# A norm worked out per 128 tokens behind bank-by-bank products, and a weight split moved by one tile

## The chip, the cores and the metric

The kernel runs on one core of a Trainium2 chip. Its time is the device time of one launch in microseconds (us); the median of three runs of the kernel before is 2459.11 us. Engines are called PE (matrix products, with its weight loads shown apart as PEld), DVE (vector), ACT (scalar activations), POOL (GpSimd) and SP (which issues most loads).

## The reference

Two transformer blocks over 256 tokens of 1024 features, all in float32. The parts that matter here are the norms that follow a product, and what reads the normed rows:

```python
def rms_norm(x, g):
    xf = x.astype(jnp.float32)
    y = xf * lax.rsqrt(jnp.mean(xf * xf, axis=-1, keepdims=True) + EPS)
    return (y * g.astype(jnp.float32)).astype(x.dtype)

def layer_norm_2(x, g, b):
    xf = x.astype(jnp.float32)
    mu = jnp.mean(xf, axis=-1, keepdims=True)
    var = jnp.mean(jnp.square(xf - mu), axis=-1, keepdims=True)
    return ((xf - mu) * lax.rsqrt(var + LN_EPS) * g.astype(jnp.float32) + b.astype(jnp.float32)).astype(x.dtype)
...
        h = h + rms_norm(merged @ w_out[i], g_mix_post[i])     # first block, then its FFN
...
        h = layer_norm_2(DN_ALPHA * h + mix, ln_mix_g[i], ln_mix_b[i])   # second block, twice
        ffn = peer_ffn(h, peer_w_q[i], peer_sub_keys[i], peer_u[i], peer_v[i])
        h = layer_norm_2(DN_ALPHA * h + ffn, ln_ffn_g[i], ln_ffn_b[i])
```

`mix` is a retention mixer in the first layer and a latent attention in the second. `peer_ffn` multiplies its input by a query weight, picks experts by product keys, and sums their rows.

## The kernel before

**Products.** Each float32 operand is split into a high half (rounded, made by ACT, line 150, tile `whi` for weights) and a low half (the rest, made by DVE, line 165, tile `wlo`); a product is three matrix multiplications. Weights come as 797 units of 128x1024 in the order of `PLAN`; SP loads them four ahead, and helpers issue the halves ahead of their use: `issue_hi` up to a limit the high half, `issue_split` the low half too, `run_ahead(1)` the low half of the next unit. The order of instructions on each engine is the order in which the Python code issues them; every engine works through its own list in that order.

**Two kinds of product.** `lin_tm` gives rows of tokens: two blocks of 128 tokens, two banks of 512 features each, so four banks, `psb[b][h]`. With `apart=True` (the products `w_out`, `r_o`, `p_v0`, `m_o`, `p_v1`) the last two weight units are multiplied bank by bank: block 0's two banks, then block 1's, six multiplications a bank. Then `issue_hi(use+2)` issues one more high half (not for `w_out` and `p_v1`), `after(psb)` works out the norm, and `keep_warm` gives PE 17 idle multiplications (line 294). `lin_fm` gives tiles of 128 features by 256 tokens; with `head=2` the first two weights are multiplied tile by tile of the input, as the input is produced, and only from the third weight on one weight at a time.

**The norm.** `LnTail.after` (lines 467 to 472) calls `ln_coeffs`: statistics of the four banks (DVE, line 392), two aggregations (394), then `rstd_root` for both blocks at once: root on ACT (368), variance plus epsilon on DVE (369), the next high half by `ahead` on ACT, reciprocal (377) and a Newton step of three operations (378 to 380), the shift `nm` (405). Then DVE scales block 1 (471) and ACT block 0 (472), half by half. `RmsTail.after` (788 to 793, for `w_out`) is the same with sums of squares by ACT (413), their addition on DVE (415), and no shift. The closing norm in `after1` (1619 to 1637, for `p_v1`) already goes block by block, with both halves of each scaled by ACT (1631); after it come gains on DVE (1635), shifts on POOL for block 0 and on DVE for block 1 (1636), and four stores (1637).

**What follows.** Behind `r_o` and `m_o` stands a query stage (`p_q0`, `p_q1`): PE transposes the normed rows tile by tile (423), ACT applies gain and shift (`rows`, 477), DVE casts the high half (`split`, 483; for tile 5 ACT does, 481) and takes the low half (484), PE multiplies by two weights. Once tile 3 (`HS`) is multiplied, `run_ahead(1)` issues the third weight's low half on DVE; by then `split` of tile 5 has been issued. Behind `p_v0` stands `m_in`, a `lin_tm` fed in the same way.

Of the kernel before, what the change touches and what calls it, by code (L numbers as in the profile page):

```python
# [10 lines left out]
F32 = mybir.dt.float32  # L11
# [4 lines left out]
AF = mybir.ActivationFunctionType  # L16
ALU = mybir.AluOpType
AX = mybir.AxisListType

P = 128  # L20
T = 256
D = 1024
KD = D // P
EPS1 = 1e-6
EPS2 = 1e-5
# [58 lines left out]
WRM = 17  # L84
WR0 = 17

HS = {"p_q0": 3, "p_q1": 3}
HA = (5,)
RSCH = ((1, 0, (0, 1, 2)), (2, 4, (4, 5, 6)), (3, 8, (8, 9, 10)))
SK = 6  # L90
GH = 1
@with_exitstack
def fused_kernel(ctx: ExitStack, tc: tile.TileContext, a: dict, out: bass.AP):
    nc = tc.nc
# [48 lines left out]
    def issue_hi(limit):  # L143
        while st["hi"] < min(limit, len(units)):
            j = st["hi"]
            issue_dma(j + 1)
            n, i, c = units[j]
            if (n, i) not in F4:
                hi = wst.tile([P, 1024], F32R, tag="whi", name=f"whi{j}", bufs=AHEAD + 1)
                nc.scalar.activation(out=hi[:, :c], in_=raws[j][:, :c], func=AF.Copy)  # L150
                his[j] = hi
            st["hi"] += 1
# [143 lines left out]
    def lin_tm(name, x_of, nk, ncol=1024, i0=0, budget=0.0, mid=None, after=None, psb=None, each=None, lead=0, warm=0, apart=False):  # L296

        if psb is None:  # L300
            psb = [[bank(0), bank(1)], [bank(2), bank(3)]]
        for k in range(nk - 2 if apart else nk):
            w = take(name, i0 + k) if k < lead else weight(name, i0 + k, budget)
            if each:
                each(k)
            if mid and k == nk - 2:
                mid(psb)
            if after and k == nk - 1:
                table_ready()
            for b in range(2):  # L310
                xs = x_of(k, b)
                for h, ps in enumerate(psb[b]):
                    tm_half(w, ps, 512 * h, *xs, ncol, k == 0, k == nk - 1)
        if apart:
            ks = (nk - 2, nk - 1)
            ws = []
            for k in ks:
                ws.append(take(name, i0 + k) if ws else weight(name, i0 + k, budget))
                if each:
                    each(k)  # L320
            mid(psb)
            table_ready()
            for b in range(2):
                for h, ps in enumerate(psb[b]):
                    for k, w in zip(ks, ws):
                        tm_half(w, ps, 512 * h, *x_of(k, b), ncol, False, k == nk - 1)
            if name not in ("w_out", PLAN[-1][0]):
                issue_hi(st["use"] + 2)
        if after:
            after(psb)  # L330
        if warm:
            keep_warm(warm)
        return psb
# [9 lines left out]
    def small(tag, n, dt=F32):  # L343
        return sm.tile([P, 8], dt, tag=tag, name=tag)[:, :n]
# [18 lines left out]
    def rstd_root(v, scale, eps, ahead=False):  # L363

        n = v.shape[-1]
        s, x = small("nm", n), small("rx", n)
        i = 0 if eps == EPS1 else 1
        nc.scalar.activation(out=s, in_=v, func=AF.Sqrt, scale=scale, bias=eps_t[:, i:i + 1])
        nc.vector.tensor_scalar(out=x, in0=v, scalar1=scale, scalar2=eps, op0=ALU.mult, op1=ALU.add)
        if ahead and GH:  # L370
            issue_hi(st["use"] + 3)
        return recip_root(s, x, n)

    def recip_root(s, x, n):

        y, t = small("ry", n), small("rt", n)
        nc.vector.reciprocal(out=y, in_=s)
        nc.vector.scalar_tensor_tensor(out=t, in0=y, scalar=-0.5, in1=y, op0=ALU.mult, op1=ALU.mult)
        nc.vector.tensor_tensor(out=t, in0=t, in1=x, op=ALU.mult)
        nc.vector.scalar_tensor_tensor(out=y, in0=t, scalar=1.5, in1=y, op0=ALU.add, op1=ALU.mult)  # L380
        return y

    def ln_coeffs(rows, eps, root=False, ahead=False):

        return coeffs_of(ln_stats(rows), eps, root, ahead)
# [75 lines left out]
    class LnTail:  # L461
# [2 lines left out]
        def __init__(self, y, g, b_, h, hl):  # L464
            self.y, self.g, self.b_, self.h, self.hl = y, g, b_, h, hl

        def after(self, psb):
            r, nm = ln_coeffs(psb, EPS2, root=True, ahead=True)
            for h in range(2):
                s_ = slice(512 * h, 512 * h + 512)  # L470
                nc.vector.tensor_scalar(out=self.y[:, 1, s_], in0=psb[1][h], scalar1=r[:, 1:2], scalar2=nm[:, 1:2], op0=ALU.mult, op1=ALU.add)
                nc.scalar.activation(out=self.y[:, 0, s_], in_=psb[0][h], func=AF.Identity, scale=r[:, 0:1], bias=nm[:, 0:1])

        def rows(self, k):
            ps = ax()
# [273 lines left out]
    for gi in range(4):  # L749
        for f in range(2):  # L750
            c = 2 * gi + f
# [30 lines left out]
    class RmsTail:  # L782
# [2 lines left out]
        def __init__(self, y, junk, g, h_in, h_out):  # L785
            self.y, self.junk, self.g, self.h_in, self.h_out = y, junk, g, h_in, h_out

        def after(self, psb):
            r = rms_coeff(psb, D, EPS1, self.junk)
            for h in range(2):  # L790
                s_ = slice(512 * h, 512 * h + 512)
                nc.vector.tensor_scalar(out=self.y[:, 1, s_], in0=psb[1][h], scalar1=r[:, 1:2], scalar2=None, op0=ALU.mult)
                nc.scalar.activation(out=self.y[:, 0, s_], in_=psb[0][h], func=AF.Copy, scale=r[:, 0:1])

        def residual(self, k):
            ps = ax()
# [277 lines left out]
    def peer(layer, hl, lt, scope, after_of, mid_of=None, beside_v=()):  # L1074
# [305 lines left out]
        last = {}  # L1380
# [14 lines left out]
            last["after"] = after_of(X)  # L1395

        bg.extend(beside_v)
        lin_tm(f"p_v{layer}", x_of, P, each=each, mid=mid, budget=0.6, after=lambda psb: last["after"](psb), warm=0 if layer else WRM, apart=True)
        return box["PE"], X

    hl2_box = {}
# [212 lines left out]
    def after1(X):  # L1614
        flat = X.rearrange("p a b -> p (a b)")
        y = flat[:, 0:2048].rearrange("p (b f) -> p b f", b=2)
        gb = gb_of(X)

        def after(psb):
            cf = []  # L1620
            for b in range(2):
                bs = sm.tile([P, 2, 2, 6], F32, tag="bs", name="bs")
                mv = sm.tile([P, 2, 2], F32, tag="mv", name="mv")
                for i, c in enumerate(psb[b]):
                    nc.vector.bn_stats(out=bs[:, 0, i, :], in_=c)
                nc.vector.bn_aggr(out=mv[:, 0, :], in_=bs[:, 0])
                cf.append(coeffs_of(mv[:, 0:1, :], EPS2, root=True))
                r, nm = cf[b]
                for h in range(2):
                    s = slice(512 * h, 512 * h + 512)  # L1630
                    nc.scalar.activation(out=y[:, b, s], in_=psb[b][h], func=AF.Identity, scale=r[:, 0:1], bias=nm[:, 0:1])
            for b in range(2):
                for h in range(2):
                    s = slice(512 * h, 512 * h + 512)
                    nc.vector.tensor_tensor(out=y[:, b, s], in0=y[:, b, s], in1=gb[:, 0, s], op=ALU.mult)
                    (nc.vector if b else nc.gpsimd).tensor_tensor(out=y[:, b, s], in0=y[:, b, s], in1=gb[:, 1, s], op=ALU.add)
                    nc.sync.dma_start(out=out[b * P:(b + 1) * P, s], in_=y[:, b, s])
        return after

    PE1, X = peer(1, hl, lt, [ML], after1, mid1)  # L1640
# [119 lines left out]
```

## Time and profile before

| | before |
|---|---|
| median of three runs | 2459.11 us (2458.69 to 2462.93) |
| profiled execution, own time | 2459.09 us |
| its span, first to last instruction | 2457.1 us |
| PE busy | 2420.2 us (98%) |
| DVE busy | 1795.3 us (73%) |
| ACT busy | 1285.8 us (52%) |
| POOL busy | 8.2 us |
| mean granted PE clock | 0.995 |

The busy times are sums over the whole span; the change concerns five short stretches around 315, 745, 1543, 1652 and 2445 us, and a piece of two query stages around 757 and 1663 us. In a time line a row is: start and length in us, engine, line, operation, output<-inputs, shapes, how many are merged into the row, and in brackets the idle time of the engine in front of it with what ended it.

### The profile page before, as it was taken

The numbers are of one execution on the slowest core, as the hardware profiler recorded it, in microseconds if no ns is written. First come the engines' busy times: TensorE is split into PE (matmuls) and PEld (weight loads), VectorE is DVE, ScalarE is ACT, GpSimd is POOL, SyncE is SP. The second block draws the span as 40 slices with busy tenths as digits, with TensorE's granted clock in tenths as the row PEclk, the third lists the DMA queues.
The fourth block names the chain that finished last, engine by engine and source line by source line (L and its number), as shares of the span: only waits on it lengthen the run. The fifth ranks groups of instructions, "written<-read, shape, count | busy, mean of one in ns | idle before, by whom it ended". The sixth has DMA issues, their size and how long they took to land. (4 is left out here: it accounts for less than half of the span.)

```text
span 2457.1 us, 43020 instructions
## 1 busy us (share of the span) xinstructions
PE 2420.2 (98%) x16811; PEld 2204.2 (90%) x16811; DVE 1795.3 (73%) x3460; ACT 1285.8 (52%) x2176; POOL 8.2 (0%) x15
## 2 busy tenths in 40 slices
PE   8999999999999999999999999999999999999998
PEld 8899989889889999999878888779999999888886
DVE  7988767767657888889655555667978898555555
ACT  5444555564455555555455455645565555454544
POOL 0000000000000000000000000000000000000000
PEclk9999999999999999999999999999999999999999
DMA  6645556646355555555555565425565555656553
GB/s 205 217 146 172 176 162 193 196 156 196 129 182 169 169 187 179 172 164 173 188 188 192 193 195 183 136 82 168 191 196 165 167 168 173 212 191 196 193 192 129
DMA packets 119772, 432.66 MB, mean 176 GB/s; under 512 B 13808, under 2 KB 14192, under 8 KB 119184
## 3 DMA queue, kind: packets, MB, share of 16 engines
q1 hardware_dynamic: 118832, 425.84, 53.5%
q0 software_dynamic: 736, 4.06, 0.5%
q8 instruction: 132, 2.16, 0.4%
q14 instruction: 72, 0.59, 0.1%
HBM read 428.81 MB, written 1.05 MB: 175 GB/s over the span
## 5 line engine op out<-in xcount | busy, mean ns | idle before, releaser
L165 DVE TENSOR_TENSOR wlo<-raw,whi 128x1024 fp32r<-128x1024 f32 (+1 forms) x797 | 970.1, 1219 | 486.8 <-ACT whi L150 484.0
L150 ACT ACTIVATE whi<-raw 128x1024 fp32r<-128x1024 f32 (+1 forms) x797 | 839.9, 1055 | 682.6 <-PE bank L288 443.4
L222 PE MATMUL bank<-hl,whi 128*128 128x256 f32 x2080 | 586.9, 282 | 4.0 <-ACT hl L569 3.0
L223 PE MATMUL bank<-hl,whi 128*128 128x256 f32 x2080 | 579.3, 279 | 0.3
L224 PE MATMUL bank<-hl,wlo 128*128 128x256 f32 x2080 | 578.7, 278 | 0.5 <-DVE wlo L165 0.5
L286 PE MATMUL bank<-whi,ch 128*128 128x512 f32 x1024 | 398.9, 390 | 2.0 <-ACT ch L340 2.0
L288 PE MATMUL bank<-whi,cl 128*128 128x512 f32 x1024 | 398.7, 389 | 0.3 <-DVE cl L341 0.2
L287 PE MATMUL bank<-wlo,ch 128*128 128x512 f32 x1024 | 398.4, 389 | 0.0
L222 PEld LDWEIGHTS bank<-hl,whi 128*128 128x128 f32 x2080 | 393.5, 189 | 5.3 <-ACT hl L569 3.3
L223 PEld LDWEIGHTS bank<-hl,whi 128*128 128x128 f32 x2080 | 392.2, 189 | 1.7 <-DVE hl L484 1.1
L224 PEld LDWEIGHTS bank<-hl,wlo 128*128 128x128 f32 x2080 | 392.2, 189 | 1.3 <-DVE wlo L165 1.0
L222 PE MATMUL lps<-hl,whi 128*128 128x256 f32 x1208 | 341.8, 283 | 1.0 <-ACT fhl L853 0.6
L224 PE MATMUL lps<-hl,wlo 128*128 128x256 f32 x1208 | 336.0, 278 | 0.5 <-DVE wlo L165 0.5
L223 PE MATMUL lps<-hl,whi 128*128 128x256 f32 x1208 | 335.9, 278 | 0.0
L286 PEld LDWEIGHTS bank<-whi,ch 128*128 128x128 f32 x1024 | 192.2, 188 | 42.4 <-ACT ch L340 2.8
L288 PEld LDWEIGHTS bank<-whi,cl 128*128 128x128 f32 x1024 | 192.2, 188 | 41.7 <-DVE cl L341 1.8
L222 PEld LDWEIGHTS lps<-hl,whi 128*128 128x128 f32 x1208 | 227.2, 188 | 1.7 <-ACT fhl L853 0.7
L224 PEld LDWEIGHTS lps<-hl,wlo 128*128 128x128 f32 x1208 | 227.7, 188 | 0.7 <-DVE wlo L165 0.7
L223 PEld LDWEIGHTS lps<-hl,whi 128*128 128x128 f32 x1208 | 227.8, 189 | 0.3
L287 PEld LDWEIGHTS bank<-wlo,ch 128*128 128x128 f32 x1024 | 192.2, 188 | 39.6
L1321 ACT ACTIVATE gel<-bank 128x16 f32<-128x16 f32 (+31 forms) x152 | 43.5, 286 | 178.5 <-PE bank L224 178.5
L1323 ACT ACTIVATE X<-bank 128x256 f32<-128x256 f32 (+25 forms) x246 | 76.6, 311 | 107.7 <-PE bank L224 107.6
(414 smaller groups left out, 2995.9 us busy)
## 6 DMA issues: line engine op xcount, KB each, us to landing
raw<-in_p_u_dram SPq DMA_DIRECT2D x256, 512.0 KB, 3.3
raw<-in_p_v_dram SPq DMA_DIRECT2D x256, 512.0 KB, 3.3
raw<-in_w_fi_dram SPq DMA_DIRECT2D x44, 512.0 KB, 4.3
raw<-in_p_q_dram SPq DMA_DIRECT2D x32, 512.0 KB, 4.1
raw<-in_w_gate_dram SPq DMA_DIRECT2D x24, 512.0 KB, 3.4
raw<-in_w_fo_dram SPq DMA_DIRECT2D x22, 512.0 KB, 4.2
raw<-in_w_conv_dram SPq DMA_DIRECT2D x16, 512.0 KB, 4.1
raw<-in_r_qk_dram SPq DMA_DIRECT2D x16, 512.0 KB, 3.4
```

The source lines that it names most:

```text
L150: nc.scalar.activation(out=hi[:, :c], in_=raws[j][:, :c], func=AF.Copy)
L165: nc.vector.tensor_tensor(out=lo[:, :c], in0=r[:, :c], in1=hi[:, :c].bitcast(F32), op=ALU.subtract)
L222: nc.tensor.matmul(ps, w[0], x[0], start=start, stop=False, skip_group_check=True)
L223: nc.tensor.matmul(ps, w[0], x[1], start=False, stop=False, skip_group_check=True)
L224: nc.tensor.matmul(ps, w[1], x[0], start=False, stop=stop, skip_group_check=True)
L286: nc.tensor.matmul(ps[:, :n], xh, w[0][:, o:o + n], start=first, stop=False, skip_group_check=True)
L287: nc.tensor.matmul(ps[:, :n], xh, w[1][:, o:o + n], start=False, stop=False, skip_group_check=True)
L288: nc.tensor.matmul(ps[:, :n], xl, w[0][:, o:o + n], start=False, stop=last, skip_group_check=True)
L1321: nc.scalar.activation(out=gl_[:, 0:td], in_=ps[:, 0:td], func=AF.Gelu)
L1323: nc.scalar.activation(out=X[:, e, td:], in_=ps[:, td:T], func=AF.Gelu)
```

## The change

The norm behind the five products is worked out for each block of 128 tokens as soon as that block's banks are done, in the order block 0, block 1; the next high half (`issue_hi`) is issued between the two. A new helper, `rstd_block`, works on one column: root, half the negative variance plus epsilon, reciprocal, and a Newton step of two operations. Of a block's two halves, `LnTail` gives DVE only the first half of block 1 and ACT the other three; `RmsTail` gives DVE the first half of each block and ACT the second. `after1` uses `LnTail` and then the gains and shifts as before. `w_fo`, which isn't `apart`, keeps the old form. `HS` goes from 3 to 2.

```diff
-HS = {"p_q0": 3, "p_q1": 3}
+HS = {"p_q0": 2, "p_q1": 2}
...
                     for k, w in zip(ks, ws):
                         tm_half(w, ps, 512 * h, *x_of(k, b), ncol, False, k == nk - 1)
-            if name not in ("w_out", PLAN[-1][0]):
-                issue_hi(st["use"] + 2)
-        if after:
+                if b and name not in ("w_out", PLAN[-1][0]):
+                    issue_hi(st["use"] + 2)
+                after(psb, b)
+        elif after:
             after(psb)
...
+    def rstd_block(v, scale, eps, ahead=False):
+        s, x, y, r = (small(t, 1) for t in ("nm", "rx", "ry", "rq"))
+        i = 0 if eps == EPS1 else 1
+        nc.scalar.activation(out=s, in_=v, func=AF.Sqrt, scale=scale, bias=eps_t[:, i:i + 1])
+        nc.vector.tensor_scalar(out=x, in0=v, scalar1=-0.5 * scale, scalar2=-0.5 * eps, op0=ALU.mult, op1=ALU.add)
+        if ahead and GH:
+            issue_hi(st["use"] + 3)
+        nc.vector.reciprocal(out=y, in_=s)
+        nc.vector.tensor_scalar(out=r, in0=y, scalar1=y, scalar2=x, op0=ALU.mult, op1=ALU.mult)
+        nc.vector.scalar_tensor_tensor(out=r, in0=r, scalar=1.5, in1=y, op0=ALU.add, op1=ALU.mult)
+        return r
...
-        def after(self, psb):
-            r, nm = ln_coeffs(psb, EPS2, root=True, ahead=True)
+        def after(self, psb, b):
+            bs = sm.tile([P, 2, 2, 6], F32, tag="bs", name="bs")
+            mv = sm.tile([P, 2, 2], F32, tag="mv", name="mv")
+            for i, c in enumerate(psb[b]):
+                nc.vector.bn_stats(out=bs[:, 0, i, :], in_=c)
+            nc.vector.bn_aggr(out=mv[:, 0, :], in_=bs[:, 0])
+            r, nm = rstd_block(mv[:, 0, 1:2], 1.0, EPS2, ahead=b == 1), small("nq", 1)
+            nc.vector.scalar_tensor_tensor(out=nm, in0=mv[:, 0, 0:1], scalar=-1.0, in1=r, op0=ALU.mult, op1=ALU.mult)
             for h in range(2):
                 s_ = slice(512 * h, 512 * h + 512)
-                nc.vector.tensor_scalar(out=self.y[:, 1, s_], in0=psb[1][h], scalar1=r[:, 1:2], scalar2=nm[:, 1:2], op0=ALU.mult, op1=ALU.add)
-                nc.scalar.activation(out=self.y[:, 0, s_], in_=psb[0][h], func=AF.Identity, scale=r[:, 0:1], bias=nm[:, 0:1])
+                if b and not h:
+                    nc.vector.tensor_scalar(out=self.y[:, b, s_], in0=psb[b][h], scalar1=r, scalar2=nm, op0=ALU.mult, op1=ALU.add)
+                else:
+                    nc.scalar.activation(out=self.y[:, b, s_], in_=psb[b][h], func=AF.Identity, scale=r, bias=nm)
...
+        def block(self, psb, b):
+            ss, x = sm.tile([P, 2, 2], F32, tag="ss", name="ss"), small("rx2", 1)
+            for i, c in enumerate(psb[b]):
+                nc.scalar.activation(out=self.junk, in_=c, func=AF.Square, accum_out=ss[:, i, 0:1])
+            nc.vector.tensor_tensor(out=x, in0=ss[:, 0, 0:1], in1=ss[:, 1, 0:1], op=ALU.add)
+            r = rstd_block(x, 1.0 / D, EPS1, ahead=b == 1)
+            for h in range(2):
+                s_ = slice(512 * h, 512 * h + 512)
+                if h:
+                    nc.scalar.activation(out=self.y[:, b, s_], in_=psb[b][h], func=AF.Copy, scale=r)
+                else:
+                    nc.vector.tensor_scalar(out=self.y[:, b, s_], in0=psb[b][h], scalar1=r, scalar2=None, op0=ALU.mult)
...
+        lt = LnTail(y, None, None, None, None)
+
+        def after(psb, b):
+            lt.after(psb, b)
+            if b:
+                for i in range(2):
+                    for h in range(2):
+                        stretch(i, h)
```

`stretch(i, h)` is the old code for gain, shift and store of one half.

## Rows read from the trace of the kernel before

**Rows 1.** The page, its first part: busy time, share of the span, instructions.
```profile
PE 2420.2 (98%) x16811; PEld 2204.2 (90%) x16811; DVE 1795.3 (73%) x3460; ACT 1285.8 (52%) x2176; POOL 8.2 (0%) x15
```

**Rows 2.** Time line of DVE, end of `r_o` and query stage `p_q0`.
```profile
743.14 0.70 DVE L392 BATCH_NORM_STATS2 bs<-bank 128x6 f32<-128x512 f32 x1 [0.66 <-PE bank L288]
...
749.60 1.22 DVE L165 TENSOR_TENSOR wlo<-raw,whi 128x1024 fp32r<-128x1024 f32 x1
...
755.40 0.43 DVE L484 TENSOR_TENSOR hl<-hm,hl 128x256 fp32r<-128x256 f32 x1 [1.26 <-ACT hl L481]
755.74 1.22 DVE L165 TENSOR_TENSOR wlo<-raw,whi 128x1024 fp32r<-128x1024 f32 x1
```

**Rows 3.** Time line of ACT, end of `r_o`.
```profile
745.18 1.06 ACT L150 ACTIVATE whi<-raw 128x1024 fp32r<-128x1024 f32 x1 [3.95 <-PE bank L288]
746.84 0.30 ACT L368 ACTIVATE nm<-mv,eps_t 128x2 f32<-128x2 f32 x1 [0.60 <-DVE mv L394]
...
748.15 1.45 ACT L472 ACTIVATE yl<-bank,nm,ry 128x512 f32<-128x512 f32 x2
749.50 2.11 ACT L477 ACTIVATE hm<-ax,vec 128x256 f32<-128x256 f32 x4
```

**Rows 4.** Time line of PE, end of `r_o` and query stage `p_q0`.
```profile
748.99 0.66 PE L423 MATMUL ax<-cst,yl 128*128 128x128 f32 x4 [0.38 <-ACT yl L472]
...
756.53 0.28 PE L224 MATMUL bank<-hl,wlo 128*128 128x256 f32 x1
757.22 0.38 PE L222 MATMUL bank<-hl,whi 128*128 128x256 f32 x1 [0.41 <-DVE hl L483]
...
759.08 0.28 PE L222 MATMUL lps<-hl,whi 128*128 128x256 f32 x1
...
761.90 0.28 PE L222 MATMUL lps<-hl,whi 128*128 128x256 f32 x1
```

**Rows 5.** Time line of all engines, the closing norm.
```profile
2443.20 0.70 DVE L1625 BATCH_NORM_STATS2 bs<-bank 128x6 f32<-128x512 f32 x1 [0.66 <-PE bank L288]
...
2445.54 1.45 ACT L1631 ACTIVATE X<-bank,nm,ry 128x512 f32<-128x512 f32 x2 [1.07 <-DVE nm L405]
...
2446.99 0.29 ACT L368 ACTIVATE nm<-mv,eps_t 128x1 f32<-128x1 f32 x1
...
2447.70 0.16 DVE L379 TENSOR_TENSOR rt<-rt,rx 128x1 f32<-128x1 f32 x1
2447.90 0.16 DVE L380 SCALAR_TENSOR_TENSOR ry<-rt,ry 128x1 f32<-128x1 f32 x1
...
2448.17 2.96 DVE L1635 TENSOR_TENSOR X<-X 128x512 f32<-128x512 f32 x3
```

**Rows 6.** Time line of all engines, end of `w_out`.
```profile
310.79 0.58 ACT L413 ACTIVATE junk<-bank 128x512 f32<-128x512 f32 x1
...
311.49 0.60 ACT L413 ACTIVATE junk<-bank 128x512 f32<-128x512 f32 x1
...
313.86 0.60 ACT L413 ACTIVATE junk<-bank 128x512 f32<-128x512 f32 x1 [0.69 <-PE bank L288]
...
314.78 0.30 ACT L368 ACTIVATE nm<-rx,eps_t 128x2 f32<-128x2 f32 x1 [0.23 <-DVE rx L415]
...
317.22 1.22 DVE L165 TENSOR_TENSOR wlo<-raw,whi 128x1024 fp32r<-128x1024 f32 x1
```

**Rows 7.** Time line of all engines, end of `p_v0`.
```profile
1539.31 0.70 DVE L392 BATCH_NORM_STATS2 bs<-bank 128x6 f32<-128x512 f32 x1 [0.66 <-PE bank L288]
...
1541.35 0.79 ACT L150 ACTIVATE whi<-raw 128x704 fp32r<-128x704 f32 x1 [3.91 <-PE bank L288]
...
1543.01 0.30 ACT L368 ACTIVATE nm<-mv,eps_t 128x2 f32<-128x2 f32 x1 [0.86 <-DVE mv L394]
```

**Rows 8.** Busy us by stretch behind `w_out`; after POOL: granted PE clock, DMA share, GB/s.
```profile
316.50:319.00 2.50, 0.81 (x6) 0.54 (x6) 2.50 (x5) 1.75 (x4) 0.00 (x0) 1.00 0.00 0
319.00:322.40 3.40, 3.40 (x16) 3.15 (x17) 2.77 (x7) 1.83 (x5) 0.00 (x0) 0.51 0.46 154
```

More of the change, by code (lines that the diff above doesn't have):

```diff
@@ L786, in __init__, with after @@
             self.y, self.junk, self.g, self.h_in, self.h_out = y, junk, g, h_in, h_out
-        def after(self, psb):
+        def after(self, psb, b=None):
+            if b is not None:
+                return self.block(psb, b)
             r = rms_coeff(psb, D, EPS1, self.junk)
@@ L1397, in peer @@
         bg.extend(beside_v)
-        lin_tm(f"p_v{layer}", x_of, P, each=each, mid=mid, budget=0.6, after=lambda psb: last["after"](psb), warm=0 if layer else WRM, apart=True)
+        lin_tm(f"p_v{layer}", x_of, P, each=each, mid=mid, budget=0.6, after=lambda psb, b: last["after"](psb, b), warm=0 if layer else WRM, apart=True)
         return box["PE"], X
@@ L1617, in after1, with stretch @@
         gb = gb_of(X)
[L1619 to L1637, printed above, removed]
+        def stretch(b, h):
+            s = slice(512 * h, 512 * h + 512)
+            nc.vector.tensor_tensor(out=y[:, b, s], in0=y[:, b, s], in1=gb[:, 0, s], op=ALU.mult)
+            (nc.vector if b else nc.gpsimd).tensor_tensor(out=y[:, b, s], in0=y[:, b, s], in1=gb[:, 1, s], op=ALU.add)
+            nc.sync.dma_start(out=out[b * P:(b + 1) * P, s], in_=y[:, b, s])
+        lt = LnTail(y, None, None, None, None)
[5 more added lines that the diff above has]
+                        stretch(i, h)
         return after
```

## The prediction

> **What bounds the kernel now.** I read the page first: the matmul engine (PE) is busy 98% of the span [rows 1]. The bulk of the kernel is therefore PE streaming, which this change does not touch. Time can be won or lost only where PE waits: at the joints where a bank-by-bank product ends, its norm is worked out, and the next product needs the normed, transposed rows. Five products go this way: `w_out`, `r_o`, `p_v0`, `m_o`, `p_v1`. For each joint I then read the time lines of DVE, ACT and PE side by side, and last the granted clock.
>
> At `r_o` block 0's second bank is measured on DVE from 743.14, while PE still works on block 1. After PE's last product the root runs at 746.84, the scalings on ACT and DVE start at 748.15, PE's transposes at 748.99 after a wait of 0.38, and at 749.60 DVE splits a weight before it may cast the first tile [rows 2 to 4]. So the first product waits for DVE: the split ends at 749.60+1.22 = 750.82, whereas ACT's rows begin at 749.50 [rows 2, 3]. Later in the same stage PE waits again, at 757.22, for a cast that stands on DVE behind the third weight's split of 755.74 [rows 2, 4]. `m_o` with the second query stage repeats this pattern (two places in all).
>
> **Part 1: the third weight's split, one tile up.** `HS` 3 to 2 puts the split behind tile 4's low half instead of tile 5's. PE goes from its last product of tile 5 (756.53) to the first of the third weight (759.08) in 2.55 us, thirteen steps; one step is (761.90-759.08)/24 = 0.1175, so 1.53 would do, and 1.02 is the stall [rows 4]. Where the split goes, DVE sits idle for 1.26 in front of tile 5's low half, waiting for ACT [rows 2]; a split takes 1.22 [rows 2]. That idle time is the cover, and if it went, the stall would merely move to an earlier tile and the gain would be 0. With it the split also frees its raw buffer some 1.3 us earlier, so one load on SP's queue is asked for earlier; nothing waits for that weight for several tiles, cost 0. The next work late would be ACT's copy for tile 5, which already set the end of the idle time. Two stages: **-2.04**, ends -2.04 and 0.
>
> **Part 2: the shorter Newton step.** Three small DVE operations become two. Such operations start 0.20 apart (2447.70, 2447.90) [rows 5]. A small operation with two pointer scalars has no row; the large scalings of the same engine take such pointers, and I take 0.20 saved, with ends 0.13 and 0.20. The second aggregation that goes saves nothing for block 1, since it has to follow the last statistics anyway.
>
> **Part 3: block 0 first, and what is queued behind it.** Block 0's chain now runs beside PE's last twelve products of block 1. The kernel before already does this at its very end: from the second statistics (2443.20) to ACT's scaling (2445.54) it takes 2.34, and the two halves keep ACT until 2446.99, when the second root starts [rows 5]. With the shorter step the offset is 2.14. On ACT the new program order is root 0, both halves of block 0, then the next weight's high half, then root 1. The high half used to run at 745.18, in ACT's idle time [rows 3]. That is the added wait: root 1 is queued behind three instructions, and DVE and PE wait for root 1.
>
> - *`r_o`.* Scaling of block 0 at 743.14+2.14 = 745.28; two halves 1.45, high half 1.06, each next start about 0.10 before the end of the one before (748.15+1.45 against 749.50): root 1 at 745.28+1.35+0.96 = 747.59, against 746.84: +0.75 [rows 2, 3]. Root to scaling was 1.31, now 1.11, so DVE scales block 1's first half at 748.70 (+0.55). DVE has one half instead of two, (749.60-748.15)/2 = 0.73 less: its weight split starts at 749.43 (-0.17) [rows 2, 3]. The transposes come 0.55 later, at about 749.54, and ACT's rows with them at about 750.0; tile 0's row is then ready near 750.6, still ahead of the split's end at 750.65. Between -0.17 and +0.55 I take **0**, because what ended last, the split, moves little and the late side has just that slack.
> - *`m_o`.* The same order and sizes: **0**, same ends.
> - *`p_v0`.* The high half is 704 wide, 0.79 [rows 7]. Scaling at 1539.31+2.14 = 1541.45, root 1 at 1541.45+1.35+0.69 = 1543.49 against 1543.01 (+0.48), less 0.20: +0.28 [rows 7]. No split stands behind the scaling on DVE here, so transposes, rows and products all move: **+0.28**, ends -0.20 and +0.50.
> - *`w_out`.* Here ACT squares the banks. Root comes 0.92 after the start of the last square (313.86 to 314.78) [rows 6]. Root 0 at 311.49+0.92 = 312.41; root to scaling is one operation shorter than at `r_o` (no shift), 1.11-0.20 = 0.91, so ACT's half of block 0 starts at 313.32 and takes about 0.60, as a square of that width; the squares of block 1 start at 313.92 and, 0.70 apart (310.79, 311.49), at 314.62; root 1 at 315.54 (+0.76) [rows 6]. DVE scales at 316.45 and, 0.73 later, splits at 317.18, against 317.22 [rows 6]: **-0.04**, ends -0.20 and +0.20.
> - *`p_v1`, the end.* Root 1 has to wait for the aggregation, which saves only about 0.11. Scaling at 2446.88+1.11 = 2447.99. DVE used to start the gains at 2448.17 [rows 5]; now it first scales half of block 1, 0.73, and starts them at 2448.72. GpSimd's shifts, DVE's last ones and the stores follow from that: **+0.55**, ends 0 and +0.75.
>
> Sum: -2.04+0+0+0.28-0.04+0.55 = -1.25. The profiled execution took 2459.09 (span 2457.1 and 2.0 around it), the median of three is 2459.11, so one sum serves both: **2457.8**.
>
> **The rivals.**
>
> *The clock falls (slower).* [...] At `r_o` PE's wait before the transposes was 0.38 and no fall followed; by my sum it becomes 0.93, and another of some 0.4 follows before the third pair of transposes. A fall costs at most 3.40 x 0.49 = 1.67 where PE is the bound. Three places (`r_o`, `p_v0`, `m_o`): 2457.8+5.0 = 2462.8; a single one, 2459.5, already outweighs the gain, so that is the point from which this rival makes the kernel slower than before. What speaks for it is that PE's waits at these joints come closer to those at `w_out`; what speaks against it is that they stay shorter. [...] Chance 0.18.
>
> *ACT's queue holds nothing up.* If the high half slips in before block 0's halves or ends early, root 1 keeps its place: the query stages gain 0.20+0.73 each and `p_v0` 0.20. That is 2x0.93+0.48 = 2.3 better: 2455.5. Against it: block 0's scaling is ready at 745.28, as ACT would otherwise be idle, and the program puts it first. Chance 0.09.
>
> *The clock at `w_out` stays up.* The transposes there come some 0.3 earlier, since they no longer need ACT's halves behind two high halves. Up to 1.67 is won back, part of it hidden by DVE and ACT: 2456.2 to 2457.8, middle 2457.0. The idle time only moves from in front of the transposes to behind them. Chance 0.11.
>
> *The moved split does not do what it says.* If it stalls an earlier tile by as much, -1.25+2.04 = +0.8: 2459.9. Against it: the 1.26 idle time [rows 2]. Chance 0.07.
>
> **How the numbers follow.** My forecast, 2457.8, has the remaining 0.55. The measurement of this kernel tells about 0.2%, 4.9 us, from no change: below 2454.2 is faster, above 2464.0 slower. Only the second and third rival together, or unnamed causes, reach the first; only three falls of the clock and more reach the second. The three executions before lie between 2458.69 and 2462.93, so a median can stray upwards by a microsecond or two. Range 2454.8 to 2461.2; it leaves out most of the three-fall case. Faster 0.04, same 0.92, slower 0.04.
>
> **What would show it.** In the profile after: PE's wait of 0.41 in the query stages' seventh tile is gone, with the third split beginning before tile 5's low half; root 1 of `r_o` and `m_o` stands on ACT behind two scalings and a high half, and starts some 0.75 later against the last product; PE's first transposes there wait about 0.9; at the end DVE's first gain starts some 0.55 later against the last product. Wrong I would be most of all if the clock's levels changed anywhere, if root 1 kept its place, or if the span moved by more than 5 us, since no row here holds that much.

## The result: 20 us slower, and the time is not at the joints

| | before | after |
|---|---|---|
| median | 2458.9 us (4 runs, 2455.7 to 2462.9) | 2481.3 us (4 runs, 2478.9 to 2487.9) |
| profiled execution, own time | 2459.09 us | 2478.86 us |
| its span | 2457.1 us | 2477.1 us |
| mean granted PE clock | 0.995 | 0.996 |

The ratio of after to before is 1.0094 (95% interval 1.0075 to 1.0113). The forecast was 2457.8 us.

The page of after, first its busy line (it answers to [rows 1]), then the rows of the big products with `ch` and `cl` in the two stages `p_v0` and `p_v1` (line engine op, output<-inputs, shape, count | busy us, mean ns of one | idle before):

```profile
PE 2439.3 (98%) x16811; PEld 2203.9 (89%) x16811; DVE 1797.4 (73%) x3472; ACT 1288.0 (52%) x2182; POOL 8.2 (0%) x15
...
L286 PE MATMUL bank<-whi,ch 128*128 128x512 f32 x1024 | 404.8, 395 | 1.9 <-ACT ch L341 1.9
L288 PE MATMUL bank<-whi,cl 128*128 128x512 f32 x1024 | 404.6, 395 | 0.1
L287 PE MATMUL bank<-wlo,ch 128*128 128x512 f32 x1024 | 404.3, 395 | 0.0
```

The same three rows on the page of before:

```profile
L286 PE MATMUL bank<-whi,ch 128*128 128x512 f32 x1024 | 398.9, 390 | 2.0 <-ACT ch L340 2.0
L288 PE MATMUL bank<-whi,cl 128*128 128x512 f32 x1024 | 398.7, 389 | 0.3 <-DVE cl L341 0.2
L287 PE MATMUL bank<-wlo,ch 128*128 128x512 f32 x1024 | 398.4, 389 | 0.0
```

PE is busy 19.1 us longer with the same 16811 instructions, and one product (one matrix multiplication) of 512 columns takes 395 ns where it took 389 or 390. The busy time of one such row overlaps with its neighbours (in before 389 to 390 ns long, 226.8 ns from start to start), so the price is better read from how many fit into a stretch. Busy us of PE and its instructions in two stretches (granted clock, DMA share and GB/s behind), one of mostly narrow products (256 columns; some 350 of 128 columns stand between them) and one in `p_v0` with wide ones (512 columns) alone; after:

```profile
900.00:1100.00 200.00, 200.00 (x1921) 1.00 0.54 175
1400.00:1500.00 100.00, 100.00 (x432) 1.00 0.58 190
```

and before:

```profile
900.00:1100.00 200.00, 200.00 (x1924) 1.00 0.54 174
1400.00:1500.00 100.00, 100.00 (x443) 1.00 0.60 194
```

The narrow stretch holds as many as ever (1921 and 1924); the wide one holds 432 instead of 443, 2.5% fewer, at a granted clock of 1.00 in both and with PE busy throughout. From here on "interval" means the time from one product's recorded start to the next one's, averaged over a stage of the trace without the few pairs that have a wait between them (over 300 ns). A product's *stationary* tile is what I call the first operand of its `matmul`, of which a row of PEld takes 128x128 ahead of the product (0.19 us, in the time line of e18 below); the *moving* one is the second, with the 512 or 256 columns of the product's own row. In the wide products the weight tile is the moving one, in the narrow ones the stationary one. By stage, first to last product:

| stage (stationary tile) | before: us, interval | after: us, interval | longer by |
|---|---|---|---|
| `w_fo` (`fhl`) | 59.6, 226.7 ns | 61.1, 232.3 ns | 1.5 us |
| `r_o` (`yhl`) | 45.2, 226.9 ns | 46.4, 233.2 ns | 1.2 us |
| `p_v0` (`ch`, `cl`) | 351.6, 226.8 ns | 360.2, 232.6 ns | 8.6 us |
| `p_v1` (`ch`, `cl`) | 349.9, 226.7 ns | 360.0, 233.3 ns | 10.2 us |

These four hold 21.5 us, more than the whole loss of 20.0 us between the two spans. The waits of DVE's low halves for `whi` (484.0 to 506.0 us) and of ACT's high halves for PE (443.4 to 462.4 us) grow by about as much. The list of PE's instructions is the same in both kernels, in the same order. What differs for these products is where their operands lie. The two new scratch names `rq` and `nq` have two buffers of 32 bytes each, 128 bytes in each partition, in the pool `sm`, and every tile allocated behind that pool lies 128 bytes higher: `X` at 74432 instead of 74304, and with it the split inputs `ch`, `cl`, `fhl`, `yhl`, `ohl`, `hl5` and `cqhl` of later products. The weights `whi` and `wlo`, and `hl`, lie ahead of the pool and stay. Within 256 bytes `whi` and `wlo` are at 64; `ch`, `cl`, `fhl`, `yhl` went from 64 to 192. I call the place of an operand minus that of `whi`, within 256 bytes, its *distance*: it was 0 and became 128.

The joints came out much as predicted. Time line of after at the end of `r_o` and in `p_q0` (it answers to [rows 2 to 4]):

```profile
747.43 0.40 PE L288 MATMUL bank<-whi,yhl 128*128 128x512 f32 x1
...
748.67 1.05 ACT L150 ACTIVATE whi<-raw 128x1024 fp32r<-128x1024 f32 x1
...
749.62 0.29 ACT L379 ACTIVATE nm<-mv,eps_t 128x1 f32<-128x1 f32 x1
...
750.14 0.27 DVE L384 TENSOR_SCALAR rq<-ry,rx 128x1 f32<-128x1 f32 x1
...
750.45 0.16 DVE L385 SCALAR_TENSOR_TENSOR rq<-rq,ry 128x1 f32<-128x1 f32 x1
750.64 0.16 DVE L488 SCALAR_TENSOR_TENSOR nq<-mv,rq 128x1 f32<-128x1 f32 x1
...
750.83 0.81 DVE L492 TENSOR_SCALAR yl<-bank,rq,nq 128x512 f32<-128x512 f32 x1
751.56 1.22 DVE L165 TENSOR_TENSOR wlo<-raw,whi 128x1024 fp32r<-128x1024 f32 x1
751.70 0.55 PE L437 MATMUL ax<-cst,yl 128*128 128x128 f32 x3 [0.98 <-DVE yl L492]
...
756.01 1.22 DVE L165 TENSOR_TENSOR wlo<-raw,whi 128x1024 fp32r<-128x1024 f32 x1
...
757.14 0.36 PE L222 MATMUL bank<-hl,whi 128*128 128x256 f32 x1
```

Root 1 does stand behind ACT's high half of 748.67, PE's first transposes wait 0.98, and the third weight's split (756.01) runs ahead of tile 5 with no wait of PE behind it.

### The profile page after: what moved, and what is told of

The parts are those of the page before. It is cut to its first block, busy times and chain, and to the rows that moved or that the text cites. A ratio compares the mean times of both kernels' runs of the same rounds, so it can differ in the third digit from the quotient of the medians.

```text
span 2477.1 us, 43039 instructions
## 1 busy us (share of the span) xinstructions
PE 2439.3 (98%) x16811; PEld 2203.9 (89%) x16811; DVE 1797.4 (73%) x3472; ACT 1288.0 (52%) x2182; POOL 8.2 (0%) x15
## 5 line engine op out<-in xcount | busy, mean ns | idle before, releaser
L165 DVE TENSOR_TENSOR wlo<-raw,whi 128x1024 fp32r<-128x1024 f32 (+1 forms) x797 | 968.4, 1217 | 508.7 <-ACT whi L150 506.0
L150 ACT ACTIVATE whi<-raw 128x1024 fp32r<-128x1024 f32 (+1 forms) x797 | 839.4, 1054 | 689.7 <-PE bank L288 462.4
L286 PE MATMUL bank<-whi,ch 128*128 128x512 f32 x1024 | 404.8, 395 | 1.9 <-ACT ch L341 1.9
L288 PE MATMUL bank<-whi,cl 128*128 128x512 f32 x1024 | 404.6, 395 | 0.1
L287 PE MATMUL bank<-wlo,ch 128*128 128x512 f32 x1024 | 404.3, 395 | 0.0
L286 PEld LDWEIGHTS bank<-whi,ch 128*128 128x128 f32 x1024 | 192.5, 188 | 48.5 <-ACT ch L341 2.8
L288 PEld LDWEIGHTS bank<-whi,cl 128*128 128x128 f32 x1024 | 192.5, 188 | 47.4 <-DVE cl L342 1.8
L287 PEld LDWEIGHTS bank<-wlo,ch 128*128 128x128 f32 x1024 | 192.5, 188 | 45.8
L224 PEld LDWEIGHTS lps<-hl,wlo 128*128 128x128 f32 x1208 | 226.9, 188 | 0.7 <-DVE wlo L165 0.7
```

The lines of the kernel that those rows point to most:

```text
L165: nc.vector.tensor_tensor(out=lo[:, :c], in0=r[:, :c], in1=hi[:, :c].bitcast(F32), op=ALU.subtract)
L224: nc.tensor.matmul(ps, w[1], x[0], start=False, stop=stop, skip_group_check=True)
L286: nc.tensor.matmul(ps[:, :n], xh, w[0][:, o:o + n], start=first, stop=False, skip_group_check=True)
L287: nc.tensor.matmul(ps[:, :n], xh, w[1][:, o:o + n], start=False, stop=False, skip_group_check=True)
L288: nc.tensor.matmul(ps[:, :n], xl, w[0][:, o:o + n], start=False, stop=last, skip_group_check=True)
```

## The experiments

Theory A: the loss is the place of the tiles, by their distance from `whi` and `wlo`. Theory B: it is the new order of instructions, which puts the engines into another rhythm that lasts through the stages behind. The numbers of all runs stand together here; "wide" is the mean interval in `p_v0` and `p_v1`, and the last column is how much the narrow products of the whole trace stand beyond 113.3 ns apart, summed (only pairs between 115 and 130 ns count). The traced run is one of those in the median.

| run | median us | ratio to before, 95% | wide ns | narrow, sum beyond 113.3 |
|---|---|---|---|---|
| before | 2457 to 2463, six medians | 1 | 226.8, 226.7 | 15.2 us |
| after | 2481.26 | 1.0094, 1.0075 to 1.0113 | 232.6, 233.3 | 16.1 us |
| e1_pad128 | 2484.54 | 1.0108, 1.0089 to 1.0126 | 233.2, 232.4 | 15.2 us |
| e2_same_place | 2459.18 | 1.0007, 0.9997 to 1.0016 | 226.8, 226.7 | 14.3 us |
| e3_hs_only | 2458.22 | 0.9999, 0.9988 to 1.0010 | 226.8, 226.7 | 15.8 us |
| e4_pad512 | 2461.22 | 1.0009, 0.9998 to 1.0019 | 226.8, 226.7 | 17.4 us |
| e5_all128 | 2487.19 | 1.0113, 1.0084 to 1.0142 | 226.9, 226.7 | 44.1 us |
| e6_w128 | 2508.80 | 1.0201, 1.0168 to 1.0234 | 232.4, 232.4 | 41.6 us |
| e7_pad256 | 2459.95 | 1.0010, 0.9996 to 1.0024 | 226.9, 226.7 | 16.8 us |
| e8_pad64 | 2488.06 | 1.0117, 1.0087 to 1.0146 | 233.3, 233.3 | 21.5 us |
| e9_hl64 | 2506.63 | 1.0198, 1.0181 to 1.0215 | 226.8, 226.7 | 64.5 us |
| e10_best | 2505.25 | 1.0193, 1.0176 to 1.0210 | 226.8, 226.7 | 67.8 us |
| e11_after_placed | 2509.32 | 1.0209, 1.0192 to 1.0226 | 226.8, 226.7 | 67.7 us |
| e12_hl32 | 2495.41 | 1.0153, 1.0133 to 1.0174 | 226.8, 226.7 | 49.8 us |
| e13_hl192 | 2499.39 | 1.0163, 1.0119 to 1.0207 | 226.8, 226.7 | 51.7 us |
| e14_hl224 | 2490.98 | 1.0129, 1.0083 to 1.0176 | 226.8, 226.7 | 43.5 us |
| e15_hl160 | 2510.55 | 1.0209, 1.0163 to 1.0254 | 226.9, 226.7 | 65.1 us |
| e16_hl96 | 2481.01 | 1.0095, 1.0073 to 1.0118 | 226.8, 226.7 | 35.7 us |
| e17_ch_cl | 2485.93 | 1.0087, 1.0070 to 1.0104 | 232.5, 233.3 | 28.6 us |
| e18_cl | 2476.02 | 1.0047, 1.0031 to 1.0064 | 231.2, 231.1 | 21.6 us |

### Place or order

e1: the kernel before and one unused tile.

```diff
+    sm.tile([P, 16], F32, tag="gap0", name="gap0")
     rt1 = RmsTail(y1, junk, "g_mix_post", xT, h1)
```

> The kernel before with one unused scratch tile of 128x16 f32 added in front of the others, so that every on-chip tile allocated after it lies 128 bytes higher in each partition, as in the kernel after; not one instruction is added, removed or moved. Theory A (the loss of 20 us comes from where the tiles lie: ch, cl, fhl, yhl, hl5 and others 128 bytes higher, whi and wlo where they were): 2476 to 2481 us, 512-wide products of p_v0 and p_v1 start 232 to 233 ns apart instead of 227, waits at the joints as in before. Theory B (the loss comes from the new order of instructions, which sets PE and the other engines in another rhythm for the stages behind): 2459 us within 2 us, 227 ns apart.

e2: the kernel after, with `r` and `nm` in spare columns of the tile `ry`.

```diff
-        s, x, y, r = (small(t, 1) for t in ("nm", "rx", "ry", "rq"))
+        s, x = (small(t, 1) for t in ("nm", "rx"))
+        t = small("ry", 3)
+        y, r = t[:, 0:1], t[:, 1:2]
...
-            r, nm = rstd_block(mv[:, 0, 1:2], 1.0, EPS2, ahead=b == 1), small("nq", 1)
+            r, nm = rstd_block(mv[:, 0, 1:2], 1.0, EPS2, ahead=b == 1)
```

> The kernel after with all its instructions in their order, but the two new scratch values kept in spare columns of an older scratch tile, so that every tile lies where it lay in before. Theory A (place of the tiles): 2455 to 2458 us, that is before less the sum of the local steps (-1.25 by the prediction, up to -3 with the clock of w_out staying up), 512-wide products 227 ns apart in p_v0 and p_v1. Theory B (order of instructions): 2479 to 2481 us, 232 to 233 ns apart.

The unused tile alone makes the kernel before as slow as after (ratio 1.0108, after 1.0094), and the kernel after without the shift is as fast as before (1.0007, its interval holds 1). From the page of e1:

```profile
PE 2440.6 (99%) x16811; PEld 2204.4 (89%) x16811; DVE 1795.3 (72%) x3460; ACT 1285.5 (52%) x2176; POOL 8.2 (0%) x15
...
L286 PE MATMUL bank<-whi,ch 128*128 128x512 f32 x1024 | 404.6, 395 | 1.9 <-ACT ch L340 1.9
```

and of e2:

```profile
PE 2417.8 (98%) x16811; PEld 2202.1 (90%) x16811; DVE 1796.7 (73%) x3472; ACT 1287.7 (52%) x2182; POOL 8.2 (0%) x15
...
L286 PE MATMUL bank<-whi,ch 128*128 128x512 f32 x1024 | 398.9, 390 | 2.0 <-ACT ch L341 2.0
```

The wide stretch of 1400 to 1500 us holds 430 products in e1 and 443 in e2:

```profile
1400.00:1500.00 100.00, 100.00 (x430) 1.00 0.59 189
1400.00:1500.00 100.00, 100.00 (x443) 1.00 0.59 195
```

The 395 ns go with the places, not with the instructions: DVE's and ACT's counts (3460 and 2176, 3472 and 2182) show that e1 has before's instructions and e2 after's. Theory B falls. e1's median lies 3.5 us above the range that A gave, e2's 1.2 us above.

e4 moves the tiles of after by 512 bytes in all instead of 128, with an unused tile of 48 columns; e7 moves those of before by 256, with 32 columns, and e8 those of before by 64, with 8. In e4:

```diff
+    sm.tile([P, 48], F32, tag="gap0", name="gap0")
     rt1 = RmsTail(y1, junk, "g_mix_post", xT, h1)
```

> The kernel after with 384 further bytes of unused scratch, so that ch, cl, fhl, yhl, hl5 and the others lie 512 bytes higher than in before. Theory A with a period of 512 bytes (what matters is the place within 512 bytes): 2455 to 2458 us, 227 ns apart. Theory A without that period (each place has its own speed): anything from 2457 to 2490. Theory B: 2479 to 2481 us.

> The kernel before, with all tiles behind the scratch tiles 256 bytes higher. It asks for the period. A period of 128 is out already (a shift of 128 was slow). If the period is 256: 2455 to 2461 us, 227 ns. If it is 512 and 256 is half way off: as slow as the shift of 128 or slower, 2476 us and more, 232 ns and more.

> The kernel before, with all tiles behind the scratch tiles 64 bytes higher. Where nearness decides (stationary and moving operand on the same 64 bytes within 512): slower than before, between 227 and 233 ns, 2459 to 2480 us. Where a coarser unit of 128 bytes decides: 227 ns, 2455 to 2461 us, since the tiles stay in it.

512 and 256 cost nothing (226.8 ns), 128 and 64 do (232 to 233.3). So for the wide products a shift by 256 or 512 bytes is as good as none, and a shift of 64 is no milder than one of 128; the expectation of something between 227 and 233 fell, and e8's median (2488.06) lies above its range. e4's median lies 3 us above its range, e7's inside it. `hl5` went the other way in e8: it came to distance 0, and `w_out`'s interval fell from 228.9 to 227.1.

### Relative or by itself, and whose place

e5 puts 128 bytes in front of the weights, so that these and all behind them move together (the first added line); e6 puts 384 bytes behind the weights too (both lines). `hl` stays in both.

```diff
     sm = ctx.enter_context(tc.tile_pool(name="sm", bufs=2))
+    wst.tile([P, 32], F32, tag="gapw", name="gapw")
...
+    sm.tile([P, 48], F32, tag="gap0", name="gap0")
     rt1 = RmsTail(y1, junk, "g_mix_post", xT, h1)
```

> The kernel before, with 128 unused bytes in front of the weights' tiles, so that raw, whi and wlo and all that is allocated after them (ch, cl, fhl, yhl, hl5) lie 128 bytes higher together; hl, allocated earlier, stays. Theory A1 (what counts is where the stationary operand lies relative to the moving one, whi or wlo): 2455 to 2461 us, p_v0 and p_v1 at 227 ns. Theory A2 (what counts is where ch, cl, fhl and yhl lie by themselves): 2476 to 2482 us, 232 to 233 ns.

> The kernel before, with 128 unused bytes in front of the weights' tiles and 384 behind them: raw, whi and wlo lie 128 bytes higher, and ch, cl, fhl, yhl and hl5 by 512, which e4_pad512 showed to be as good as none. A1 (relative place): the distance is changed by 128 again, the other way: slow, 2470 to 2482 us, 230 to 233 ns in p_v0 and p_v1. A2 (place of the stationary operand alone): 2455 to 2461 us, 227 ns.

In e5 `ch` and `cl` lie where they made after slow, but the weights moved with them, and `p_v0` and `p_v1` run at 226.9 and 226.7 ns; in e6 `ch` and `cl` are back at 64, the weights at 192, and they run at 232.4. The distance counts, not the place. The times, though, fit no theory: e5 was expected at 2455 to 2461 and took 2487.19, e6 at 2470 to 2482 and took 2508.80. The stretches of e5 show why (narrow, then wide):

```profile
900.00:1100.00 200.00, 200.00 (x1865) 1.00 0.49 170
1400.00:1500.00 100.00, 100.00 (x443) 1.00 0.57 194
```

Wide is as before (443), but the narrow stretch holds 1865 instead of 1924. The weights moved away from `hl`, whose distance went from 192 to 64, and the narrow products cost 44.1 us beyond 113.3 ns apart instead of 15.2: they depend on the place too.

e17 moves only `ch`, `cl` and the scratch around them (the first added line), e18 only `cl` and what lies behind it (the other two):

```diff
             box["pp"] = PE.enter_context(tc.tile_pool(name=f"pp{layer}", bufs=1))
+            box["pp"].tile([P, 32], F32, name="gapc")
...
+            if f == 1:
+                pp.tile([P, 32], F32, name="gapl")
             q = pp.tile([P, T], F32, tag=("o1", "ohh", "ohl")[f % 3], name="q", bufs=2)
```

> The kernel before with 128 unused bytes behind X in the two peer layers: ch and cl (and the scratch of the selection behind X) lie 128 bytes higher, X, fhl, yhl, hl5 and cqhl where they were. If the distance between a product's own two operands counts: p_v0 and p_v1 at 232 to 233 ns, fhl and yhl at 227 as in before, 2474 to 2479 us. If it is another tile that moved in the kernel after (X, the smaller scratch): 227 ns throughout, 2459 us.

> As e17_ch_cl, but ch stays where it was and only cl (with the tiles behind it) lies 128 bytes higher. If the distance of the operands that PE reads at the same time counts: one of the three products in each group slows down, by about 6 ns, most likely the one during whose stream cl is loaded (wlo with ch), and the others stay at 227: p_v0 and p_v1 at about 229 ns, 2463 to 2469 us. If ACT's write of ch or any other access counts: all three at the same speed, 227 or 232 ns, 2459 or 2479 us.

In e17 `fhl` and `yhl`, not moved, keep 226.8 and 226.9 ns, and `ch`, `cl` run at 232.5 and 233.3: it is the products' own operands, not `X`. In e18 the page tells the three kinds of wide product apart:

```profile
L288 PE MATMUL bank<-whi,cl 128*128 128x512 f32 x1024 | 406.8, 397 | 0.2 <-DVE cl L341 0.2
L287 PE MATMUL bank<-wlo,ch 128*128 128x512 f32 x1024 | 405.4, 396 | 0.0
L286 PE MATMUL bank<-whi,ch 128*128 128x512 f32 x1024 | 399.0, 390 | 1.9 <-ACT ch L340 1.9
```

PE goes round L286, L287, L288, and the weight load of `cl` is recorded beside the product of L287; time line of PE and PEld in e18:

```profile
1300.12 0.39 PE L286 MATMUL bank<-whi,ch 128*128 128x512 f32 x1
1300.12 0.19 PEld L287 LDWEIGHTS bank<-wlo,ch 128*128 128x128 f32 x1
1300.35 0.40 PE L287 MATMUL bank<-wlo,ch 128*128 128x512 f32 x1
1300.35 0.19 PEld L288 LDWEIGHTS bank<-whi,cl 128*128 128x128 f32 x1
1300.58 0.40 PE L288 MATMUL bank<-whi,cl 128*128 128x512 f32 x1
1300.58 0.19 PEld L286 LDWEIGHTS bank<-whi,ch 128*128 128x128 f32 x1
```

L286, with `ch` loaded ahead of it and `ch` loaded beside it, keeps 390 ns, just as in before (intervals 226.9 and 226.7); L287 and L288, the one beside which `cl` is loaded and the one that uses it, take 396 and 397 (232.4 and 234.2). I had expected one of the three to slow down; two do, hence 231.2 ns on average instead of 229, and 2476.02 us instead of 2463 to 2469. Both medians also lie higher because the runs of before beside them do (2462.72). In both traces, besides, more narrow products stood at their slower speed (28.6 and 21.6 us against 15.2), which no theory here expected: some 6 us of it between 326 and 690 us, in e17 a further 8 us in `p_u0`, the stage behind `p_q0`. The traced run of e17 (2492.09) is the slowest of its four.

With nothing of these products moved but `cl`, the two kinds of product around its load are 6 to 7 ns slower (396 and 397 against 390), and one of them, L287, has both of its own operands where they were. Why the load of `cl` goes with a slower product beside it, no run here shows.

### The narrow products, and whether a better placing exists

In before 3292 of 10344 narrow products stood more than 115 ns apart and cost 15.2 us. If distance 0 were best for them as well, that time could be had. e9 puts 64 bytes in front of `hl` and fills up to 256 in front of the weights; e12 to e16 do the same with 8, 48, 56, 40 and 24 columns in front of `hl`.

```diff
     hm = keep.tile([P, KD, T], F32, name="hm")
+    keep.tile([P, 16], F32, name="gaph")
...
+    wst.tile([P, 48], F32, tag="gapw", name="gapw")
```

> The kernel before, with 64 unused bytes in front of hl and 192 more in front of the weights: hl, up to now 64 bytes off whi and wlo within 256, lies on the same place within 256 as these; all else keeps its distance. In before 3292 of the 10344 products of 256 columns stood more than 115 ns apart (mostly 117 to 118 instead of 113.3), 15.2 us in all, and the products of 512 columns with hl 229 instead of 226.7. Theory A1 (distance within 256 bytes, zero is best, for both widths): all at 113.3 and 226.7, about 2443 us. Rival A3 (the narrow products' second speed has nothing to do with the place, or their best distance is the one they have): 2456 to 2461 us or more, as many narrow products at 117 to 118.

> As e9_hl64, and hl5, hlp and cqhl also placed at the distance zero, and HS at 2. A1: the gain of e9_hl64, some 0.5 us for the further tiles and 2.04 us for HS: about 2440 us. A3: 2457 us.

> The kernel after with the same placing as e10_best. A1: e10_best plus what the joints of the change cost in the traces of e2_same_place against e3_hs_only (0.38 at p_v0, 0.7 at the end, 0.05 at the others): about 2441 us, 38 us below the kernel after with not one instruction changed. A3: 2457 us.

> As e9_hl64, but hl 32 bytes off whi and wlo within 256. If every distance but zero costs: between 2450 and 2485 us, most narrow products at 117 to 118. If a distance below 64 bytes counts as zero: as e9_hl64, about 2443 us.

The expectations of a gain fell, and e12 lies above both of its ranges. In e9 the wide products with `hl` did get faster (`w_pin` from 229.1 to 227.0 ns), but the narrow stretch of e9 holds 1823 instead of 1924:

```profile
900.00:1100.00 200.00, 200.00 (x1823) 1.00 0.48 166
1400.00:1500.00 100.00, 100.00 (x443) 1.00 0.57 195
```

Most narrow products there stand 120 ns apart (8695 of 10350 pairs). e10 and e11 (e9's placing with `hl5`, `hlp`, `cqhl` at distance 0, on before with `HS` 2 and on after) carry the same load; e11 against e10 adds 4 us, where I had expected 1: its trace has two more falls of the clock (at 325 and 1690 us; mean granted clock 0.994, e10's 0.996). To the 47th product behind `w_out` it takes 17.37 us where e10 takes 16.01, behind `m_o` 14.03 where e10 takes 12.43: 3.0 us, which with the two joints of the change (0.39 and 0.67) make up the 4. What is best for the wide product is not best for the narrow one, in which the weight is stationary and `hl` moves. Four more distances:

> The kernel before with hl 192 bytes higher and the weights and all behind them 256 bytes higher, so that hl lies 128 bytes from whi and wlo within 256 (before: 192; e9_hl64: 0; e5_all128: 64). If the distance rules the 256-wide products and half the period is their best: all at 113.3 ns, 15 us less there, and hl's 512-wide products at 232 to 233 ns, 2 us more: about 2446 us. If the narrow products merely suffer from every change of hl's place: 117 to 121 ns, 2475 to 2505 us.

> As e13_hl192 with hl at a distance of 160 bytes, between e13_hl192 and before. If the distance rules smoothly between 128 and 192: narrow products mostly at 113.3 ns, 2446 to 2458 us. If not: 2475 us and more.

> As e13_hl192 with hl at a distance of 96 bytes, between e13_hl192 and the 64 of e5_all128, where narrow products stood 117.7 ns apart. If the distance rules smoothly: between 113.3 and 117.7 ns, 2446 to 2487 us. If not: as slow as e5_all128 or slower, 2485 us and more.

> As e13_hl192 with hl at a distance of 32 bytes, between zero (e9_hl64, 2506 us) and 64 (e5_all128, 2487 us). If the distance rules smoothly: 118 to 120 ns, 2487 to 2506 us, close to its mirror image in e12_hl32 (2495 us). If not: anything else.

| distance of `hl` | 0 (e9) | 32 (e16) | 64 (e5) | 96 (e15) | 128 (e13) | 160 (e14) | 192 (before) | 224 (e12) |
|---|---|---|---|---|---|---|---|---|
| narrow, sum beyond 113.3, us | 64.5 | 35.7 | 44.1 | 65.1 | 51.7 | 43.5 | 15.2 | 49.8 |
| wide with `hl` (`w_pin`), ns | 227.0 | 233.3 | 233.4 | 234.1 | 232.3 | 233.3 | 229.1 | 233.3 |

All four came out as the second alternative of their expectation: there is no smooth law in it. Of eight distances the one in before is the best for the narrow products, by 20 us at least. It was no accident of e9's other shifts, since `ch` and `cl` kept their distance in all of them (226.7 to 226.9). Whether the distance counts for narrow products, or the place by itself, these runs do not separate. The tile `hlp` hints at the distance: at 64 its products stand 117.8 ns apart both in after, where `hlp` moved, and in e6, where the weights did. No run here shows a placing that beats before.

### The parts by themselves

e3: the kernel before with one number changed.

```diff
-HS = {"p_q0": 3, "p_q1": 3}
+HS = {"p_q0": 2, "p_q1": 2}
```

> The kernel before with HS at 2 and nothing else changed (the tiles lie as in before). The prediction's first part: 2457.0 us (-2.04, 1.02 in each query stage), the wait of 0.41 in the seventh tile of p_q0 and p_q1 gone. Rival: the stall moves to an earlier tile, 2459 us. Theories A and B differ little here: both leave the 512-wide products at 227 ns.

The median can't tell it from before (0.9999, 0.9988 to 1.0010). The trace can: from `r_o`'s last product to the 47th product of the query stage it is 13.40 us in before and 12.38 in e3; behind `m_o` 13.42 and 12.35. (The first two weights make 48 products, so the 47th lies behind the stall that `HS` is about.)

## Why the prediction was wrong

The step that failed is the first: "The bulk of the kernel is therefore PE streaming, which this change does not touch." The instructions of that bulk were not touched; their operands were. The prediction costed every instruction of the two new names and gave the names themselves no cost. 128 bytes of scratch moved `ch`, `cl`, `fhl` and `yhl` to distance 128, and 3072 products of `p_v0` and `p_v1` got 5.8 and 6.6 ns longer each, 8.9 and 10.1 us; together that is nine times the largest term of the sum (2.04). The last sentence of the prediction, that no row holds more than 5 us, followed from the same gap: the rows showed what the products cost at the place that they had.

The steps of the sum itself hold, read from the traces of e2 (all local parts, places of before) and e3 (`HS` alone), from the last product of a joint:

| term | predicted | measured |
|---|---|---|
| `HS`, two stages | -2.04 | -1.02 and -1.07: -2.09 (e3 against before) |
| shorter step, small operations alone | -0.20 | about -0.10 |
| `r_o` to the 47th product behind | 0 | +0.06 (e2 against e3) |
| `m_o`, likewise | 0 | +0.03 |
| `p_v0` to the first product of `m_in` | +0.28 | +0.38 (5.32 to 5.70) |
| `w_out` to the 47th product behind | -0.04 | +0.03 (16.01 to 16.04) |
| `p_v1`, last product to first gain | +0.55 | +0.67 (2.68 to 3.35) |
| sum without the second line, which is in the others | -1.25 | -0.92 |

- *Part 1* is right to 0.05 a stage. The split of 756.01 takes the idle time that was named for it, and nothing new waits.
- *Part 2* was mis-sized, and outside its bounds of 0.13 to 0.20. The operation with two pointer scalars, for which before had no row, lasts 0.27 and the next starts 0.31 behind it (750.14, 750.45), then 0.19 (750.64). That is 0.50 for two operations where three took 0.60.
- *Part 3, `r_o`*. Root 1 behind the last product: 746.84-745.44 = 1.40 before, 749.62-747.43 = 2.19 after, +0.79 where +0.75 was predicted. The scaling moved by 0.69 instead of 0.55: 0.04 from the root, 0.10 because the step saved less. The split moved by -0.03 instead of -0.17, for the same reason. The end result, close to 0, is as predicted.
- *`p_v0` and the end* are 0.10 and 0.12 later than predicted, about the 0.10 of Part 2. At the end DVE does scale half a block before the gains, in the time line of after:

```profile
2464.79 0.40 PE L288 MATMUL bank<-whi,cl 128*128 128x512 f32 x1
...
2466.20 0.29 ACT L379 ACTIVATE nm<-mv,eps_t 128x1 f32<-128x1 f32 x1
...
2467.42 0.81 DVE L492 TENSOR_SCALAR X<-bank,rq,nq 128x512 f32<-128x512 f32 x1
...
2468.15 2.95 DVE L1658 TENSOR_TENSOR X<-X 128x512 f32<-128x512 f32 x3
```

From the last product to the first gain it is 3.36, against 2448.17-2445.49 = 2.68 in before ([rows 5] has the gain).

*The rivals.* A fall of the clock is meant as in [rows 8], whose 3.40 us at a granted 0.51 are the terms of the first rival's 1.67. That a longer wait of PE brings one was my assumption, which no run shows. In the trace of after the granted clock was 1.00 around `r_o`, `p_v0` and `m_o` (740 to 760, 1535 to 1560 and 1640 to 1680 us), although PE waited 0.98, 0.70 and 0.98 there; in e2 the stretches behind them took only 0.06, 0.38 and 0.03 us longer (table above). In e11, which has the same joints, it did fall in the stage behind `m_o` (0.57 granted from 1690 to 1694 us), which cost 1.60 us against e10; the prediction had said at most 1.67. But e5 and e13, whose joints are those of before, lost about as much there (14.98 us to the 47th product in both, 13.42 in before), so the first rival is neither confirmed nor ruled out. In after the clock stayed up behind `w_out` (1.00), as the third rival had it. The stretch that [rows 8] lie in, busy us by engine and then the granted clock, in after:

```profile
316.00:323.00 7.00, 5.18 (x37) 3.88 (x36) 6.03 (x15) 4.87 (x11) 0.00 (x0) 1.00 0.23 75
```

in before, and in e3, whose `w_out` is before's:

```profile
316.00:323.00 7.00, 5.31 (x30) 4.38 (x28) 5.77 (x11) 4.08 (x9) 0.00 (x0) 0.76 0.22 75
316.00:323.00 7.00, 5.70 (x45) 5.08 (x46) 5.51 (x12) 4.41 (x11) 0.00 (x0) 1.00 0.23 75
```

e3 keeps a granted clock of 1.00 there with no change to the joint; e11, with the change, has its fall at 325 us and takes 17.37 us to the 47th product. So the change did not do it: the fall there differs from trace to trace and is worth about 1.1 us (17.15 in before against 16.01 in e3 to the 47th product). Root 1 did wait in ACT's queue, so the second rival did not happen, nor the fourth.

Of the change it is left that its two scratch names are worth +20 us and its instructions, by the steps read from single traces, some -0.9. The medians do not show that gain: e2's ratio of 0.9997 to 1.0016 means -0.7 to +3.9 us.

## What to carry to other kernels

A new tile moves every tile that is allocated behind it, and in this kernel, with PE busy for 98% of the span, that cost 20 us, more than any step of the change: look up the places before and after, and keep the distance between the operands of the big products, or keep a new value in a spare column of an old tile. When PE's busy time changes with the same list of products, compare how many fit into an equal stretch before looking for waits. To tell place from order, run the old kernel with an unused tile of the new size, and the new kernel with the old places.

## What was not expected of the hardware

- In the traces here, wide products (512 columns) whose two operands are at distance 0 within 256 bytes follow each other at 226.7 to 227.1 ns in the stages of 95 products and more (only `m_o`, which waits cut into pieces, has 229.5 to 230), at the other distances at 228.8 to 234.2. Narrow ones (256 columns) stand 113.3 ns apart at best, and with `hl` they were slowest, 119.7 ns on average, at distances 0 and 96.
- At distance 192 these traces show two speeds in one and the same kernel: wide products with `hl` at 229 or 233 ns from stage to stage and from run to run (`w_pin` 229.1 in before, 233.4 in after, with none of its operands moved), narrow ones at 113.3 or 117 to 118. What decides between them stays open. With it go the 6 to 13 us that e8, e17 and e18 have more in the narrow products than before, with `hl` and the weights where they were.
- A small DVE operation of one column with two pointer scalars lasts 0.27 us (ten of them in after), the others of one column in that norm 0.15 to 0.17.
